# One decoder layer on 256 tokens: TensorE's order written in the source, side work as chains, both token halves on one weight pair, p's projection first

## The chip, the cores and the metric

The kernel runs on one core of a Trainium2 chip. The metric is the device time of one execution in microseconds (us), the median of several runs of the same program; lower is better.

## The reference

One layer of a hybrid decoder, for 256 tokens of width 2048, in float32. Cut to what matters:

```python
h = rms_norm(x, g_mix_pre);  proj = h @ w_in                     # 2048 x 9728
aq, ak, av, hq, hf, hi, hg, gate_a, gate_b = split(proj)
y_attn = sliding_window_attention(rotary(aq), rotary(ak), av, attn_sinks)
o      = hgrn2_recurrence(hq, hf, hi, lb)       # log_f = log(lb + (1-lb) sigmoid(hf)), chunks
y_hgrn = rms_norm(o, hgrn_gnorm) * silu(hg)
merged = sigmoid(gate_a) * (y_attn @ w_attn_branch) + sigmoid(gate_b) * (y_hgrn @ w_hgrn_branch)
x = x + rms_norm(merged @ w_out, g_mix_post)
gate, up = split(rms_norm(x, g_ffn_pre) @ w_gate_up)             # 2048 x 11264
x = x + rms_norm((silu(gate) * up) @ w_down, g_ffn_post)         # 5632 x 2048
ple_gate = sigmoid(rms_norm(x, g_ple_pre) @ w_ple_gate)          # 2048 x 2048
x = x + rms_norm((p @ w_ple_proj) * ple_gate, g_ple_post)        # p is 256 x 256
```

Rotary takes sine and cosine of position times a frequency; the positions come as int32.

## The kernel before, in words

**Products.** The 256 tokens are two halves, c = 0 and 1, of 128 tokens each. An activation is kept transposed (128 rows of the inner dimension by 128 tokens), and a float32 product x @ w is made as three products of the fp32r type, xh·wh + xh·wl + xl·wh, where xh and wh are rounded and xl and wl are the remainders. A weight tile `raw` is a pair of chunks of 128 rows by 512 columns, 512 KB, loaded on SyncE's queue (`weight_load`). `weight_split` makes `wh` on ScalarE (a copy) and `wl` on VectorE (a subtraction). There are 5 buffers for raw and 8 for each of wh and wl. A block of 512 output columns with an inner dimension of 2048 takes 8 such pairs. `products` (L123) runs all 8 pairs for one half, 48 wide matmuls (128 by 512) into one PSUM tile `acc` (four buffers); `block` does half 0, evacuates it, then half 1. The splits of all 8 pairs are thus held until half 1 has used them.

**Order before.** The program is written stage by stage and a scheduler orders each engine's instructions by priority. Splits get a priority of 1000 instructions ahead (AHEAD), the two steps `apply` (residual, norm and new transposes behind w_out and w_down) 3000 (URGENT). Only the first block is pinned (`kept`, `pinned`): there instructions stay in the order of the source.

**Stages.** (1) The first block of w_in (HGRN's forget gate, `hf`), whose products run as pieces of x arrive. Per piece (512 columns of one half): four transposes into `misc`, the gain, hi and lo. `lower_bounds` makes `lb` by a round trip through DRAM (`lbd`), and `oml` is 1 − lb. (2) The other 18 blocks of w_in, the mixer. Beside them run `rotary_tables` (26 small VectorE steps on a tile `rot`, from `posi`, the positions, cast to `posf`), the four HGRN chains `hgrn_core(c, g)` and the four attention chains. An HGRN chain has seven levels: VectorE subtracts two `bT` slices, ScalarE takes Exp, VectorE multiplies by `qT` and `kT`, TensorE multiplies into `misc` (L463, L478, L480), VectorE copies into `scT`; at its end stand the products with `v` (L516, L518) and the sums `o`. (3) The branch products, merged and transposed, and w_out. (4) SwiGLU: for each of 11 column groups j a gate block and an up block; `sg` is silu(gate), times up (L92), then four transposes (L159) and a copy to `actT`. (5) w_down, with the splits of actT. (6) p's projection: w_ple_proj has two chunks of rows, so one pair and 6 wide matmuls per half and 512 columns, each run just ahead of the w_ple_gate block that it is multiplied with; then the last norm and the stores.

PSUM has 8 banks: four acc, two `misc` with tag mt and two with mh. All small matmuls and transposes go to misc. 59 slots of 2 KB per partition hold the rest, handed out in the order of the source. The lines that matter are L123 (`products`), L159 (`transpose4`), L318 (the cast), L81, L84, L88, L89, L92 (the helpers act, tt, ts, stt, through which nearly every ScalarE and VectorE instruction goes).

Of the kernel before, what the change touches and what calls it, by code (L numbers as in the profile page):

```python
# [18 lines left out]
P = 128  # L19
# [10 lines left out]


@with_exitstack
def block_kernel(ctx: ExitStack, tc: tile.TileContext, I, out: bass.AP):
    """256 tokens as two halves of 128 on the partitions; weights stream once.

    A product x @ w is xh@wh + xh@wl + xl@wh, with xh, wh the float32r
    roundings and xl, wl the remainders (exact in float32r).
    """
# [9 lines left out]

    def nm(s):
# [22 lines left out]
    def misc(tag="mt"):  # L72
        return psum.tile([P, NB], F32, tag=tag, bufs=2, name=nm("misc"))

    pinned = [False]

    def kept(ins):
        return tc.keep_in_program_order(ins) if pinned[0] else ins

    def act(o, i, f, **kw):  # L80
        return kept(A.activation(o, i, f, **kw))  # L81

    def tt(o, a, b, op):
        return kept(V.tensor_tensor(o, a, b, op))  # L84

    def ts(o, a, s1, op0, s2=None, op1=None):
        if op1 is None:
            return kept(V.tensor_scalar(o, a, s1, None, op0))  # L88
        return kept(V.tensor_scalar(o, a, s1, s2, op0, op1))  # L89

    def stt(o, a, s, b, op0, op1):
        return kept(V.scalar_tensor_tensor(o, a, s, b, op0, op1))  # L92
# [14 lines left out]
    def weight_split(raw):  # L107
        """hi and lo parts of two k-chunks."""
# [13 lines left out]

    def products(ps, lhs, pairs, start=True, stop=True):  # L123
        n = len(pairs)
        for i, (k, parts) in enumerate(pairs):
            for j, (wh, wl) in enumerate(parts):
                xh, xl = lhs(k + j)
                T.matmul(ps, xh, wh, start=start and i == 0 and j == 0, stop=False)  # L128
                T.matmul(ps, xh, wl, start=False, stop=False)  # L129
                T.matmul(ps, xl, wh, start=False, stop=stop and i == n - 1 and j == 1)  # L130

    def block(w, ks, col, lhs, evac):
        pairs = weight_slab(w, ks, col)
        for c in range(2):
            ps = acc()
            products(ps, lhs[c], pairs)
            evac(c, ps)

    def lookup(groups):
        def f(k):  # L140
            hi, lo = groups[k // 4]
            return hi[:, k % 4, :], lo[:, k % 4, :]
        f.groups = groups
        return f
# [11 lines left out]
    def transpose4(src, tag="mt"):  # L156
        ps = misc(tag)
        for i in range(4):
            T.transpose(ps[:, cols(i)], src[:, cols(i)], ident)  # L159
# [21 lines left out]
    class Normed:  # L181
        """Transposed x * gain as hi and lo parts, and 1 / rms per token."""

        def __init__(self, gcol0):
            self.gcol0, self.groups, self.ss = gcol0, [], small("ss", 4)

        def square(self, g, xt):
            square_sum(self.ss[:, g:g + 1], xt)
# [17 lines left out]
        def done(self):  # L206
            return lookup(self.groups), rstd(self.ss, 4, D)

    def normed(xg, gcol0):
        n = Normed(gcol0)  # L210
        for g in range(4):
            n.square(g, xg[g])
            n.add(xg[g])
        return n.done()

# [1 line left out]
    x2 = I["x"].rearrange("o (c p) d -> (o c) p d", p=P)  # L217

# [6 lines left out]
    nc.sync.dma_start(ident, I["c_ident"])  # L225
    gcol = cst.tile([P, 64], F32, name="gcol")
# [5 lines left out]
    def gain_columns(names, at):  # L232
# [6 lines left out]
        ps = misc("mh")  # L239
        tc.keep_in_program_order(T.transpose(ps[:, :n], row[:n, :P], ident[:n, :n]))  # L240
        tc.keep_in_program_order(V.tensor_copy(gcol[:, at:at + n], ps[:, :n]))
        free(row)

    gain_columns(["g_mix_pre"], 0)
# [14 lines left out]
    dram = ctx.enter_context(tc.tile_pool(name="dram", bufs=1, space=bass.MemoryType.DRAM))  # L259
    lbs, oml = [slot("lb"), slot("lb")], [slot("oml"), slot("oml")]  # L260

    def lower_bounds():
        """Softmax over the two rows of logits, spread to all partitions."""
# [6 lines left out]
        kept(V.reciprocal(lm, lm))  # L270
# [3 lines left out]
        for g in range(2):  # L274
            G.dma_start(lbs[g], lbd[4 * g:4 * g + 4, :].rearrange("c p -> (c p)").partition_broadcast(P))
        free(lrow)

    # first block of w_in, its products as the halves of x arrive
    w_in = I["w_in"].rearrange("o k n -> (o k) n")
    K16 = list(range(16))  # L280
    xin = [[], []]
# [3 lines left out]
    def first_group(g):  # L285
        xin[0].append(load_x(0, g))
        raws = [weight_load(w_in, 4 * g + 2 * i, 5 * NB) for i in range(2)]
        xin[1].append(load_x(1, g))
        norms[0].add(xin[0][g], False)
        pairs = [(4 * g + 2 * i, weight_split(raws[i])) for i in range(2)]  # L290
        norms[1].add(xin[1][g], False)
        return pairs

    pinned[0] = True
    pairs = first_group(0)
    for g in range(4):
        ahead = first_group(g + 1) if g < 3 else None
        if g == 1:
            lower_bounds()
        for c in range(2):  # L300
            products(first[c], lookup(norms[c].groups), pairs, g == 0, g == 3)
# [621 lines left out]
```

## Time and profile before

| what | value |
|---|---|
| median of 3 runs | 1553.84 us (1553.49 to 1553.97) |
| span of the profiled execution | 1552.4 us |
| TensorE busy | 1516.8 us (98%), 7006 records |
| VectorE busy | 889.8 us (57%) |
| ScalarE busy | 786.3 us (51%) |
| GpSimd busy | 24.4 us (2%) |
| moved by DMA | 282.54 MB, mean 182 GB/s |

The profile has a record for each instruction of each engine. Its page gives busy times and groups: a group's row names the line, the engine, the operation, the tiles (out<-in), the shape, how often, busy time and mean duration, then the idle time ahead of the group and what ended it. PEld is TensorE's loading of the stationary side. The time of one run lies 1.44 us above the span. The row of a window gives start and end, its length, TensorE's busy time with the number of records, then the granted clock, the share of the DMA engines and GB/s; asked of all engines it lists PE, PEld, DVE, ACT and POOL in this order. A row of the timeline gives start, duration, engine, line, operation, tiles, shapes and, in brackets, the wait ahead of it with what ended it. A row of the waits gives total us, times and the longest. A float32 matmul leaves two records, an fp32r one or a transpose one.

### The profile page before, as it was taken

Reading aid. Unit: us, or ns where it says so; the run is one execution under the profiler, and the core shown is the slowest. Engines: PE = TensorE matmul, PEld = TensorE weight load, DVE = VectorE, ACT = ScalarE, POOL = GpSimd, SP = SyncE. Lnnn points to the kernel's source line nnn. Section 1 sums busy time; section 2 is a strip of 40 time slices with the busy share of each in tenths; the row PEclk is TensorE's granted clock in tenths of the full one; section 3 lists DMA queues with packets and bytes.
Section 4 is the critical chain, followed back from the end, with each engine's and each line's share of the span. In section 5 each row is a group of like instructions: output and inputs, shape, how many; then the busy total and the mean of one; then the engine's idle time right before and its main releaser. Section 6 shows DMA issues by size and latency. Waiting matters only on the chain.

```text
span 1552.4 us, 18678 instructions
## 1 busy us (share of the span) xinstructions
PE 1516.8 (98%) x7006; PEld 1243.8 (80%) x7006; DVE 889.8 (57%) x1228; ACT 786.3 (51%) x1052; POOL 24.4 (2%) x36
## 2 busy tenths in 40 slices
PE   7999999999999999999999999999999999999997
PEld 5778887887878888887888888888888888888886
DVE  6886748676445565556543553454446556654854
ACT  4755745555664433546443444344345545543852
POOL 2000000000000000000000000000000000000000
PEclk9999999999999999999999999999999999999998
DMA  7645454545336765545545654565565565755452
GB/s 245 230 135 191 129 197 139 187 129 196 110 109 210 247 211 173 193 153 196 200 162 180 217 174 168 200 219 180 172 215 190 190 195 180 246 184 179 171 179 98
DMA packets 146618, 282.54 MB, mean 182 GB/s; under 512 B 9136, under 2 KB 9600, under 8 KB 146528
## 3 DMA queue, kind: packets, MB, share of 16 engines
q1 hardware_dynamic: 145968, 280.33, 54.2%
q0 software_dynamic: 528, 1.01, 0.3%
q8 instruction: 55, 0.90, 0.2%
q14 instruction: 35, 0.29, 0.1%
q10 hardware_dynamic: 32, 0.01, 0.0%
HBM read 279.21 MB, written 2.10 MB: 181 GB/s over the span
## 4 chain that ended last, share of the span: by engine, by line
PE 83%; DMA 6%; ACT 4%; DVE 4%; issue 2%; POOL 0%; SPq 0%; POOLq 0%; ACTq 0%; DVEq 0%
PE acc L130 26%; PE acc L129 26%; PE acc L128 26%; DMA raw<-in_w_gate_up 3%; ACT wh L81 3%; PE misc L159 2%; DMA raw<-in_w_in 2%; DVE wl L84 2%; PE misc L478 1%; PE misc L599 1%; PE misc L617 1%; DVE sg L92 1%; DMA x<-in_x 1%; ACT junk L81 0%; DMA raw<-in_w_down 0%
## 5 line engine op out<-in xcount | busy, mean ns | idle before, releaser
L84 DVE TENSOR_TENSOR wl<-raw,wh 128x1024 fp32r<-128x1024 f32 x516 | 626.7, 1223 | 352.9 <-ACT wh L81 322.4
L129 PE MATMUL acc<-wl,hi 128*128 128x512 f32 x2064 | 809.7, 392 | 1.5 <-DVE wl L84 1.5
L128 PE MATMUL acc<-wh,hi 128*128 128x512 f32 x2064 | 809.4, 392 | 1.2 <-ACT hi L81 0.8
L130 PE MATMUL acc<-wh,lo 128*128 128x512 f32 x2064 | 809.1, 392 | 0.0
L81 ACT ACTIVATE wh<-raw 128x1024 fp32r<-128x1024 f32 x516 | 545.1, 1061 | 254.6 <-PE acc L130 182.1
L128 PEld LDWEIGHTS acc<-wh,hi 128*128 128x128 f32 x2064 | 388.1, 188 | 81.2 <-ACT hi L81 1.1
L129 PEld LDWEIGHTS acc<-wl,hi 128*128 128x128 f32 x2064 | 388.0, 188 | 80.9 <-DVE wl L84 2.1
L130 PEld LDWEIGHTS acc<-wh,lo 128*128 128x128 f32 x2064 | 388.0, 188 | 79.0 <-issue 0.5
L81 ACT ACTIVATE actT<-misc 128x512 f32<-128x512 f32 x22 | 13.2, 598 | 114.1 <-PE misc L159 114.1
L92 DVE SCALAR_TENSOR_TENSOR sg<-acc,rstd,sg 128x512 f32<-128x512 f32 x26 | 19.4, 747 | 77.4 <-PE acc L130 76.1
L81 ACT ACTIVATE sg<-acc,rstd 128x512 f32<-128x512 f32 x26 | 17.7, 681 | 84.1 <-PE acc L130 84.1
L84 DVE TENSOR_TENSOR lo<-actT,hi 128x512 fp32r<-128x512 f32 x44 | 30.2, 688 | 29.1 <-PE acc L129 22.1
L81 ACT ACTIVATE hi<-actT 128x512 fp32r<-128x512 f32 x44 | 27.4, 626 | 35.7 <-PE acc L130 29.8
L81 ACT ACT_TABLE_LOAD x30 | 38.5, 1283 | 2.1 <-PEq L911 1.2
L81 ACT ACTIVATE junk<-acc 128x512 bf16<-128x512 f32 x16 | 9.5, 596 | 56.2 <-DVE yg L84 56.2
L178 POOL TENSOR_TENSOR rstd<-mse,mhalf 128x1 f32<-128x1 f32 (+1 forms) x14 | 13.7, 979 | 1409.0 <-DVE mse L89 1409.0
L84 DVE TENSOR_TENSOR yg<-acc,gp 128x512 f32<-128x512 f32 x16 | 11.0, 686 | 42.7 <-PE acc L130 42.7
L81 ACT ACTIVATE xx<-xx 128x512 f32<-128x512 f32 (+1 forms) x28 | 16.7, 599 | 29.7 <-DVE xx L84 24.9
L81 ACT ACTIVATE gate<-acc,rstd 128x512 f32<-128x512 f32 x16 | 10.9, 681 | 35.1 <-PE acc L130 35.1
L605 DVE CUSTOM_DVE_ANT_0 s<-misc,amask 128x128 f32<-128x128 f32 (+1 forms) x32 | 10.1, 354 | 27.4 <-PE misc L599 27.4
L159 PE MATMUL misc<-ident,x 128*128 128x128 f32 x96 | 15.9, 296 | 8.8 <-DMA x<-in_x 6.7
L159 PEld LDWEIGHTS misc<-ident,x 128*128 128x128 f32 x96 | 11.6, 150 | 13.6 <-DMA x<-in_x 7.2
(157 smaller groups left out, 579.5 us busy)
## 6 DMA issues: line engine op xcount, KB each, us to landing
raw<-in_w_gate_up SPq DMA_DIRECT2D x176, 512.0 KB, 5.1
raw<-in_w_in SPq DMA_DIRECT2D x152, 512.0 KB, 5.1
raw<-in_w_down SPq DMA_DIRECT2D x88, 512.0 KB, 5.5
raw<-in_w_out SPq DMA_DIRECT2D x32, 512.0 KB, 5.5
raw<-in_w_ple_gate SPq DMA_DIRECT2D x32, 512.0 KB, 5.8
raw<-in_w_attn_branch SPq DMA_DIRECT2D x16, 512.0 KB, 5.9
raw<-in_w_hgrn_branch SPq DMA_DIRECT2D x16, 512.0 KB, 5.6
x<-in_x SPq DMA_DIRECT2D x16, 256.0 KB, 6.9
```

What stands on the lines that cost most here:

```text
L81: return kept(A.activation(o, i, f, **kw))
L84: return kept(V.tensor_tensor(o, a, b, op))
L92: return kept(V.scalar_tensor_tensor(o, a, s, b, op0, op1))
L128: T.matmul(ps, xh, wh, start=start and i == 0 and j == 0, stop=False)
L129: T.matmul(ps, xh, wl, start=False, stop=False)
L130: T.matmul(ps, xl, wh, start=False, stop=stop and i == n - 1 and j == 1)
L159: T.transpose(ps[:, cols(i)], src[:, cols(i)], ident)
L178: G.tensor_tensor(r, u, mhalf[:, :m], ALU.pow)
L478: T.matmul(ps[:, cols(h, 64)], xh, blk(xh)[:, :, 1, :], start=True, stop=True)
L599: T.matmul(ps[:, cols(i, nk * P)], qT[:, cols(j0 + i)], kTp[n][:, g, 0:nk * P], start=True, stop=True)
L605: V.tensor_tensor_reduce(s[:, cols(i, nk * P)], ps[:, cols(i, nk * P)], amask[:, (1 - c) * P:256], 1.0, NEG, ALU.add, ALU.max, mx[:, hb + ...
L617: T.matmul(y[:, cols(hb + i, 64)], pT[:, cols(i * nk + b)], vtok[:, b, kv:kv + 64], start=b == 0, stop=b == nk - 1)
```

## The change

1. **TensorE's order.** Each matmul and transpose is kept in the order of the source (`mm`, `transpose`). The other engines stay with the scheduler; the pinning of VectorE and ScalarE at the start, and of the cast of the positions, is gone. `products` and the new `both` advance a `clock` by 0.227 per wide and 0.11 per small matmul.
2. **Chains.** Side work (HGRN, attention, transposes behind an evacuation, apply) becomes generators. `yield d` hands back until TensorE's clock is d further; `pump`, called behind each pair of a half, runs what is due. `hurry(done)` runs waiting chains at once until a condition holds. It stands before the second group of HGRN chains, before the second pair of attention chains, in `lookup`, and where a result is needed.
3. **Both halves on one pair.** `both` runs a pair for half 0 and half 1 before the next pair; `halves_apart` keeps the old order for five blocks: the last of w_out and of w_down, SwiGLU's first gate block, the first and the last of w_ple_gate. The three terms now come as xh·wh, xl·wh, xh·wl.
4. **p's projection first.** Its four blocks open the program. The results are copied out (half 0 on ScalarE, half 1 on VectorE), stored to DRAM `projd` on GpSimd's queue, and loaded again on SyncE's queue among the weights behind w_down's start (the w_ple_gate stage multiplies by them).
5. **Smaller things.** x's first pieces are split chunk by chunk (`by_chunk`: four hi with the gain on ScalarE, four lo on VectorE, 128 by 128) as all later ones were; misc has three buffers with tag mt and one my; the mixer's blocks come in another sequence.

```diff
+    def mm(*a, t=SMALL, **kw):
+        clock[0] += t
+        tc.keep_in_program_order(T.matmul(*a, **kw))
...
+    def pump():
+        while waiting and waiting[0][0] <= clock[0]:
+            _, _, gen, pri = heapq.heappop(waiting)
+            step(gen, pri)
+
+    def hurry(done):
+        while not done():
+            _, _, gen, pri = heapq.heappop(waiting)
+            step(gen, pri)
...
+    def terms(ps, lhs, k, parts, start, stop):
+        xh, xl = lhs(k)
+        wh, wl = parts
+        mm(ps, xh, wh, t=WIDE, start=start, stop=False)
+        mm(ps, xl, wh, t=WIDE, start=False, stop=False)
+        mm(ps, xh, wl, t=WIDE, start=False, stop=stop)
...
+    def both(pss, lhs, w, ks, col, start=True, stop=True):
+        for i, k in enumerate(ks[::2]):
+            (_, parts), = weight_slab(w, [k, k + 1], col)
+            for c in range(2):
+                for j in range(2):
+                    terms(pss[c], lhs[c], k + j, parts[j], start and i == 0 and j == 0,
+                          stop and k + 2 > ks[-1] and j == 1)
+                pump()
...
         posf = small("posf", 2)
-        tc.keep_in_program_order(V.tensor_copy(posf, posi))
+        V.tensor_copy(posf, posi)
...
+    def ev_p(n):
+        def f(c, ps):
+            t = slot("proj")
+            act(t, ps, AF.Copy) if c == 0 else V.tensor_copy(t, ps)
+            G.dma_start(projd[c][n], t)
+            free(t)
+        return f
+
+    for n in range(4):
+        block(w_pp, [0, 1], n * NB, [p_lookup(0), p_lookup(1)], ev_p(n))
+        if n == 1:
+            load_xg(0)
+        if n == 2:
+            add_xg(0)
+    free(*pT)
+    lower_bounds()
+    hT = [lookup(n.groups) for n in norms]
+    for g in range(4):
+        both(first, hT, w_in, [4 * g, 4 * g + 1], 5 * NB, g == 0, False)
+        if g < 3:
+            load_xg(g + 1)
+            add_xg(g + 1)
+        both(first, hT, w_in, [4 * g + 2, 4 * g + 3], 5 * NB, False, g == 3)
...
+        factors(0)
+        for lev in range(7):
+            yield 5.5
+            if lev < 6:
+                factors(lev + 1)
+            scores(lev)
...
     mixer_block(8, evac_hi(1))
     free(*lbs, *oml)
-    hgrn_core(0, 1)
+    hurry(lambda: (1, 0) in hg_o)
+    chain(hgrn(1))
     mixer_block(0, evac_q(0))
...
         def ev_u(c, ps):
-            t = sg[c]
-            stt(t, ps, r2[c], t, ALU.mult, ALU.mult)
-            actT[c][j] = slot("actT")
-            act(actT[c][j], transpose4(t), AF.Copy)
-            free(t)
+            def f():
+                t = sg[c]
+                stt(t, ps, r2[c], t, ALU.mult, ALU.mult)
+                yield 5.0 + c
+                actT[c][j] = slot("actT")
+                act(actT[c][j], transpose4(t), AF.Copy)
+                free(t)
+            chain(f())
...
+    proj = [[slot("proj") for _ in range(4)] for _ in range(2)]
+    for n in range(4):
+        for c in range(2):
+            nc.sync.dma_start(proj[c][n], projd[c][n])
```

How it moves the instructions, at three places. **VectorE at the start of the program**, before (`h`, `lo` belong to x's first pieces, `wl` to w_in):

```order
L241 COPY gcol<-misc_80 128x16
L84 TENSOR_TENSOR h_117<-misc_112,gcol 128x512
L84 TENSOR_TENSOR lo_120<-h_117,hi_119 128x512
L84 TENSOR_TENSOR wl_124<-raw_106,wh_123 128x1024
L84 TENSOR_TENSOR wl_128<-raw_108,wh_127 128x1024
```

and after (`lrow` is the softmax of lower_bounds, `lo_89` and `wl_129` belong to p's projection, `rot` to the rotary tables):

```order
L303 COPY gcol<-misc_94 128x16
L396 CAST posf_891<-posi 128x2
L121 TENSOR_TENSOR lrow_97<-lrow_97 8x128
L125 TENSOR_SCALAR rot_893<-ctri_99,posf_891 128x32
L333 RECIPROCAL lrow_97<-lrow_97 8x128
L121 TENSOR_TENSOR wl_129<-raw_126,wh_128 128x1024
L121 TENSOR_TENSOR lo_89<-misc_83,hi_88 128x512
L121 TENSOR_TENSOR wl_155<-raw_152,wh_154 128x1024
```

The cast stood in row 71 before and stands in row 5 now, ahead of the first split; the rotary steps follow it between the splits and the chunks of x.

**TensorE in the mixer, at the end of the HGRN chain of half 1, first group**, before (`xx` are the factors of levels 4 and 5, acc_1415 is a block of w_in):

```order
L128 MATMUL acc_1415<-wh_1405,hi_292 128x512
L478 MATMUL misc_1303<-xx_1261 128x64 x4
L129 MATMUL acc_1415<-wl_1406,hi_292 128x512
L480 MATMUL misc_1314<-xx_1262 64x64 x4
L130 MATMUL acc_1415<-wh_1405,lo_293 128x512
```

and after (levels 3 to 6, then the first product with `v`):

```order
L60 MATMUL acc_1596<-wl_1756,hi_463 128x512
L60 MATMUL misc_1780<-xx_1578 128x64 x4
L60 MATMUL misc_1791<-xx_1577 128x64 x4
L60 MATMUL misc_1802<-xx_1578 64x64 x4
L60 MATMUL misc_1809<-xx_1577 64x64 x4
L60 MATMUL misc_1822<-v_889,scT_550 128x128
L60 MATMUL misc_1822<-st_1487,xx_1578 128x128
```

The wide matmuls that stood between the levels have gone to other places; these levels wait for nothing but their own chain. Elsewhere in the mixer two levels of a chain have 30 wide matmuls between them.

**TensorE at the end of a SwiGLU block**, before (acc_5951 is the up block of half 1, begun five rows earlier, and sg_5793 belongs to half 0):

```order
L128 MATMUL acc_5951<-wh_5848,hi_5629 128x512
L129 MATMUL acc_5951<-wl_5849,hi_5629 128x512
L159 MATMUL misc_5945<-ident,sg_5793 128x128 x4
L130 MATMUL acc_5951<-wh_5848,lo_5630 128x512
L128 MATMUL acc_5951<-wh_5854,hi_5629 128x512
```

and after (acc_6150 and acc_6151 are the next gate block, sg_5940 is half 0):

```order
L60 MATMUL acc_6151<-wh_6172,lo_5837 128x512
L60 MATMUL acc_6151<-wl_6173,hi_5836 128x512
L64 MATMUL misc_6189<-ident,sg_5940 128x128 x4
L60 MATMUL acc_6150<-wh_6197,hi_5699 128x512
L60 MATMUL acc_6150<-wh_6197,lo_5700 128x512
```

The transposes stood 5 wide matmuls behind half 0's last product and stand 24 behind the block's last one.

More of the change, by code (lines that the diff above doesn't have):

```diff
@@ L1 @@
+import heapq
 import math
@@ L206, in done @@
         def done(self):
[L207 to L214, printed above, removed]
+            hurry(lambda: self.squared == 4)
+            return rstd(self.ss, 4, D)
     x2 = I["x"].rearrange("o (c p) d -> (o c) p d", p=P)
+    dram = ctx.enter_context(tc.tile_pool(name="dram", bufs=1, space=bass.MemoryType.DRAM))
     def load_x(c, g):
@@ L283, in block_kernel @@
     first = [acc(), acc()]
[L285 to L299, printed above, removed]
-        for c in range(2):
-            products(first[c], lookup(norms[c].groups), pairs, g == 0, g == 3)
-        pairs = ahead
@@ L527, in hgrn_core, with hgrn @@
         hg_o[c, g] = o, rstd(ss, 1, P, 4)
+    def hgrn(g):
+        for c in range(2):
+            yield 3.0
+            yield from hgrn_core(c, g)
     def evac_hg(g):
@@ L783, in act_parts @@
     def act_parts(pair, gi):
+        hurry(lambda: all(actT[c][j] is not None for c in range(2) for j in kgroups[gi]))
         parts = [{j: split(actT[c][j]) for j in kgroups[gi]} for c in range(2)]
```

411 lines of the change are left out of this document (237 added, 174 removed).

## The prediction

> **What bounds the kernel now.** I read the page's header and groups first.
>
> ```profile
> span 1552.4 us, 18678 instructions
> PE 1516.8 (98%) x7006; PEld 1243.8 (80%) x7006; DVE 889.8 (57%) x1228; ACT 786.3 (51%) x1052; POOL 24.4 (2%) x36
> L84 DVE TENSOR_TENSOR wl<-raw,wh 128x1024 fp32r<-128x1024 f32 x516 | 626.7, 1223 | 352.9 <-ACT wh L81 322.4
> L129 PE MATMUL acc<-wl,hi 128*128 128x512 f32 x2064 | 809.7, 392 | 1.5 <-DVE wl L84 1.5
> L81 ACT ACTIVATE wh<-raw 128x1024 fp32r<-128x1024 f32 x516 | 545.1, 1061 | 254.6 <-PE acc L130 182.1
> ```
>
> TensorE is the bound: three lines of 2064 wide matmuls (128x512) make 6192. The 392 ns overlap; the pitch comes from the timeline of a full stretch, where six pitches lie between these starts:
>
> ```profile
> 793.27 0.39 PE L129 MATMUL acc<-wl,hi 128*128 128x512 f32 x1
> ...
> 794.63 0.39 PE L129 MATMUL acc<-wl,hi 128*128 128x512 f32 x1
> ...
> 795.38 0.42 PEld L159 LDWEIGHTS misc<-ident,sg 128*128 128x128 f32 x4 [0.78 <-DVE sg L92]
> ```
>
> 1.36 / 6 = 0.2267 us, and 6192 of them are 1404 us. A small matmul into `misc` takes 0.11: two and two more start 0.22 apart.
>
> ```profile
> 317.13 0.38 PE L516 MATMUL misc<-v,scT 128*128 128x128 f32 x2
> ...
> 317.35 0.39 PE L518 MATMUL misc<-st,xx 128*128 128x128 f32 x2
> ```
>
> The change keeps every wide and every small one. The pitch does not depend on which of the three terms follows which, so the new order of the terms is worth 0. What an order can change is TensorE's idle time. I find it by stage, from the windows (first the matmuls into acc, then those into misc):
>
> ```profile
> 13.40:52.75 39.35, 35.65 (x142) 1.00 0.79 264
> 52.75:160.00 107.25, 92.60 (x382) 1.00 0.48 161
> 240.00:480.00 240.00, 197.69 (x789) 1.00 0.44 148
> 480.00:720.00 240.00, 233.22 (x1014) 1.00 0.58 192
> 720.00:1200.00 480.00, 470.53 (x2050) 1.00 0.57 191
> 1200.00:1460.00 260.00, 255.37 (x1119) 1.00 0.60 194
> 1460.00:1541.90 81.90, 81.90 (x363) 1.00 0.45 154
> ```
>
> ```profile
> 52.75:160.00 107.25, 20.40 (x147) 1.00 0.48 161
> 240.00:480.00 240.00, 62.64 (x422) 1.00 0.44 148
> 480.00:720.00 240.00, 9.87 (x64) 1.00 0.58 192
> 720.00:1200.00 480.00, 13.20 (x84) 1.00 0.57 191
> 1200.00:1460.00 260.00, 6.06 (x40) 1.00 0.60 194
> ...
> L599 PE MATMUL misc<-kTp,qTa 128*128 128x256 f32 x32 | 9.3, 386 | 1.2 <-ACT qTa L81 1.2
> ```
>
> Stall of a stage = its length − acc x 0.2267 − misc x 0.11. That gives 4.5 us for 52.75 to 160; 14.7 for 240 to 480, or 11.2 once its 32 scores of 256 columns (L599) are charged 0.22; 3.1 for branches and output projection (480 to 720); 6.1 for SwiGLU (720 to 1200); 1.9 for the down projection (1200 to 1460); nothing for the last 82 us. The whole prize behind the start is thus some 27 us.
>
> **The start.** The program now runs p's projection (48 wide) and then w_in's first block (96) before anything else. Before, those first 144 wide matmuls (2 before 13.4 and 142 in the row above) were done at 52.75. So 52.75 is the mark to beat. The order of VectorE decides it. The cast `posf` from `posi` now stands ahead of the first `wl` of all.
>
> ```profile
> 4.30 0.76 POOL L258 DMA_DIRECT2D posi<-in_positions  x1
> posi<-in_positions POOLq DMA_DIRECT2D x1, 1.0 KB, 7.8
> 12.12 0.78 PE L128 MATMUL acc<-wh,hi 128*128 128x512 f32 x1
> lb<-lbd POOLq DMA_DIRECT2D x2, 256.0 KB, 4.3
> L92 DVE SCALAR_TENSOR_TENSOR lo<-misc,gcol,hi 128x128 fp32r<-128x128 f32 x64 | 19.8, 344 | 4.2 <-ACT hi L81 3.9
> L92 DVE SCALAR_TENSOR_TENSOR rot<-rot 128x64 f32<-128x64 f32 x9 | 1.9, 223 | 0.2
> ```
>
> POOL's queue up to posi is as before: it is issued at 4.3 and lands 7.8 later, at 12.1. With the cast, one row of `rot` and a reciprocal behind it, the first wl starts near 13.6 and the first `lo` of p ends at 13.6 + 1.2 + 0.7 = 15.5. TensorE's second matmul waits for that. Its own work from there (144 x 0.2266, 32 transposes of x x 0.11, a little at the low clock) would end near 53, no later than before. But VectorE cannot keep up. From row 11 of its new order to the last chunk of x's `lo` (row 109) stand 17 wl x 1.223 = 20.8 us, 32 lo x 0.344 = 11.0, four copies of p's projection (no such row before; between a 0.42 and the 0.69 of a 512-wide operation; I take 0.69) 2.8, two `oml` 0.8, 41 rows of rot and rope at about 0.2 = 8.2, and ten of norms at about 0.13 = 1.3: 44.9 us in all. Starting at 15.5 it ends at 60.4 if it never waits. It does wait: the copies for TensorE, `oml` for `lb`, whose loads now stand on POOL's queue among the stores of p's projection (4.3 us to landing), the chunks for ScalarE's `hi`. I put 2.5 us on that: the first block ends at 63, which is **+10 us**. Bounds: 53 (0, if VectorE kept pace) and 75 (+22, if it were busy only 75% of that stretch). Splits of the next block are among these rows, but TensorE's lost time is not got back by having them early.
>
> **The mixer** held 4.5 + 11.2 = 15.7 us. In the new order the levels of HGRN's chains mostly stand 30 wide (6.8 us) apart. Before, the same steps ran in a heap, with wide matmuls between them:
>
> ```profile
> 307.62 1.00 PE L478 MATMUL misc<-xx 128*128 128x64 f32 x8
> ...
> 311.10 1.08 PE L478 MATMUL misc<-xx 128*128 128x64 f32 x8
> ...
> 315.49 0.68 PE L480 MATMUL misc<-xx 128*64 128x64 f32 x8
> ```
>
> From level 3 (307.62) to level 6 (315.49) three steps take 7.9 us there, 2.6 each, so 6.8 us is enough for nearly all. But `hurry` empties the first chain before hgrn(1) enters: levels 3 to 6 of half 1 and the product behind them stand back to back, with nothing wide between. That product began at 317.13 (L516, quoted first), so from level 3 on the chain needed 9.5 us; TensorE's own part is about 2.7 (two such groups of 1.0 and two of 0.7, their overlapping ends taken off), so about 7 us stand still (5 to 10). Then 2.5 us (0 to 5) where the second hf's evacuation meets the end of half 0, because VectorE's rows there add up to about 17 us by the means of their groups where TensorE has about 15 of work. For every other chain I leave 3.5 us, as much as the head of the old chains cost:
>
> ```profile
> PE misc L159 <- ACT bT L81: 3.6, 4, 1.3
> ```
>
> 7 + 2.5 + 3.5 = 13, so **−3 us** (from −8 to +4).
>
> **SwiGLU.** The transposes of a block now stand 24 and 30 wide matmuls behind its last one, 5.4 and 6.8 us; before they stood 5 and 8 behind the last of their half.
>
> ```profile
> PE misc L159 <- DVE sg L92: 3.9, 10, 0.7
> ...
> PE acc L129 <- DVE wl L84: 1.5, 2, 0.8
> ```
>
> The waits name 3.9 us in 10 places for it, the stage shows 6.1; the last sg of a block is done 0.78 us after TensorE's loads began to wait, so with 5 us it always is there: **−5.5 us** (−3.9 to −6.1). The branches' transposes, the chains of the two applies and the down projection hold 3.1 + 1.9 = 5.0 us, of which I take **−3.5** (0 to −5.0): w_out's and w_down's last blocks still run half after half, so half 0's norm lies under half 1's 48 matmuls as before.
>
> **At nothing.** Both halves on one pair: a pair now serves 12 matmuls at once, 2.72 us, against 1.22 us of VectorE and 1.06 of ScalarE for its split; TensorE's waits for wl before are 1.5 us in two places. DMA: 512 KB per 2.72 us is 193 GB/s; 264 GB/s moved at the start. p's projection adds 2 MB of stores on POOL's queue and 2 MB of loads on SP's queue among w_down's weights, where 194 GB/s moved; five raw buffers and eight split pairs lie between queue and TensorE. Without that cover 2 MB would cost 2 / 0.194 = 10 us, and at the very end nothing waits for it. After the last matmul (1541.9) nothing changes: 10.5 us.
>
> **Sum.** 1552.4 + 10 − 3 − 5.5 − 3.5 = 1550.4 us of span. The runs' median of 1553.84 is 1.4 over the profiled span, so **1551.8 us**. A measurement can tell about 0.2% (3.1 us) from no change; this is inside it.
>
> **Rivals.** (1) *Chains in time*: VectorE's rows overlap at their ends and the chunks come before TensorE needs them; the block ends at 57.5 and hurry costs 5: 1551.8 − 5.5 − 2 = 1544.3. For it: many of the small rows are independent. Against it: nothing but order stands between cast, splits and chunks. (2) *VectorE's start falls behind*, slower: if waits in its fixed order leave it busy 80% of the stretch, the block ends at 15.5 + 44.9 / 0.8 = 71.6, 8.6 later than forecast: 1560.4. It decides once the block ends after 68.2 (busy share under 85%). For it: in 13.4 to 52.75 VectorE was busy
>
> ```profile
> 13.40:52.75 39.35, 36.62 (x164) 29.09 (x163) 28.07 (x39) 23.97 (x36) 2.23 (x4) 1.00 0.79 264
> ```
>
> 28.07 of 39.35 us, 71%. Against it: it had less to do then. (3) *The clock falls.* After its long first wait TensorE ran at a pitch of 0.42, and came to 0.22 at about 15.5 (the granted clock of the windows reads 1.00 there too, so the pitch has to show it):
>
> ```profile
> 14.40 0.63 PE L128 MATMUL acc<-wh,hi 128*128 128x512 f32 x1
> ...
> 14.82 0.61 PE L129 MATMUL acc<-wl,hi 128*128 128x512 f32 x1
> ...
> 15.51 0.39 PE L128 MATMUL acc<-wh,hi 128*128 128x512 f32 x1
> ...
> 15.73 0.39 PE L129 MATMUL acc<-wl,hi 128*128 128x512 f32 x1
> ```
>
> From 12.12 to 15.5 that lost about half, 1.7 us. No later wait before exceeds 1.3 us; if two stalls of the new order (the start, hurry) were long enough to drop the clock again, 2 x 1.5 = 3 us come on top: 1554.8. The Trainium skill, "TensorE: Matmul & The Clock Gate", Part 1, states such a gate: half clock after about 3.4 us without work, full again after about 3.4 us of work; it speaks against packing dependent rows with nothing between, and by it the price would be an estimated 1.7 us a gap. The rows above agree with the warm-up; no row before shows a fall later on.
>
> **Chances.** Forecast 0.40 (1547 to 1557), rival 1 0.25, rival 2 0.27, rival 3 0.08. Faster by over 0.2% (under 1550.7): rival 1 and 0.17 of the forecast, 0.42. Within 0.2%: 0.23 of the forecast and rival 3, 0.31. Slower: 0.27. The range goes from the start at no cost (1541.8) to a VectorE busy 75% there (block's end at 75.4: 1564.2); the forecast alone spans 1547 to 1557.
>
> **What would show it.** In the changed profile: the first 144 wide matmuls end near 63 and TensorE's waits at the start name VectorE's lo and wl; one stretch of about 11 us in the mixer with no acc matmul between five misc groups; no wait for sg in SwiGLU, a stage stall there under 1 us; a pitch of 0.22 to 0.23 everywhere behind 19 us. Wrong if the block ends before 57 or after 68, if SwiGLU keeps over 2 us of stall, or if w_down shows waits for proj or raw.

## The result, and the profile after

The changed kernel takes 1582.86 us (median of 4 runs, 1580.27 to 1583.53) against 1553.9 us for the kernel before: 1.0175 times as long, 95% interval 1.016 to 1.0191. The forecast was 1551.8 us with a range to 1564. The profiled execution took 1580.27 us, 2.2 over its span; it is the fastest of the four.

The head of the page after, and of its 40 slices (39.5 us each) TensorE's busy tenths and its granted clock:

```profile
span 1578.1 us, 18723 instructions
PE 1521.9 (96%) x7006; PEld 1260.5 (80%) x7006; DVE 889.0 (56%) x1248; ACT 789.7 (50%) x1070; POOL 24.7 (2%) x44
...
PE   5999989999999999997999999999999999999897
...
PEclk9999989999999999998999999999999999999999
```

Slices 6 and 19 (from 197 and from 710 us) show less work and a lower clock together, slice 38 (from 1460) and the first less work. The waits of TensorE after:

```profile
PE misc L64 <- DVE x L129: 14.3, 2, 8.1
PE acc L60 <- DVE lo L129: 6.2, 4, 4.4
PE acc L60 <- DVE lo L121: 5.1, 1, 5.1
PE acc L60 <- ACT hi L118: 4.0, 1, 4.0
...
PE misc L60 <- DVE xx L121: 3.4, 2, 3.0
PE misc L64 <- DVE kTp L682: 3.3, 2, 2.0
```

The work is the same (7006 records); TensorE waits more, and for VectorE. The two waits for `x`, 14.3 us together, are new: the residual that is transposed behind w_out and behind w_down. No wait for `sg` is left. (Each row: total, times, longest.)

The windows by stage, with TensorE's wide matmuls, cut where each stage's last one has begun (96 or 144 in the first, 1728 in the mixer, 384 in the branches, 384 in w_out, 2112 in SwiGLU, 1056 in w_down, the rest; a record or two at an edge is counted twice). After:

```profile
0.00:66.42 66.42, 40.42 (x144) 0.95 0.81 265
66.42:547.37 480.95, 414.64 (x1730) 0.99 0.54 160
547.37:637.12 89.75, 87.86 (x386) 1.00 0.67 209
637.12:726.49 89.37, 88.16 (x386) 1.00 0.56 167
726.49:1227.49 501.00, 487.53 (x2114) 0.99 0.65 191
1227.49:1468.72 241.23, 240.46 (x1058) 1.00 0.63 198
1468.72:1567.49 98.77, 90.49 (x386) 0.97 0.44 141
```

And before, by the same stages:

```profile
0.00:39.30 39.30, 24.96 (x96) 1.00 0.75 247
39.30:519.07 479.77, 418.73 (x1730) 1.00 0.49 163
519.07:610.38 91.31, 89.01 (x386) 1.00 0.69 223
610.38:700.64 90.26, 87.84 (x386) 1.00 0.53 178
700.64:1198.05 497.41, 485.88 (x2113) 1.00 0.56 188
1198.05:1441.14 243.09, 240.19 (x1058) 1.00 0.61 196
1441.14:1542.15 101.01, 99.28 (x434) 1.00 0.46 157
```

The second number of a row is the stage's length; that is where to read. p's 48 wide matmuls (10.9 us) moved from the last stage to the first. Put at the same place they leave: start 66.42 − 39.30 − 10.9 = +16.2, mixer +1.2, branches −1.6, w_out −0.9, SwiGLU +3.6, w_down −1.9, w_ple_gate 98.77 − 101.01 + 10.9 = +8.7, the tail +0.4. The sum is the 25.7 us by which the span grew. Two stages that should have gained have lost, SwiGLU and w_ple_gate, both at their head. This is the timeline behind w_out's last block, which ends at 726.5 (VectorE's and TensorE's rows that matter):

```profile
729.60 0.40 PE L60 MATMUL acc<-wl,hi 128*128 128x512 f32 x1
...
734.75 0.68 DVE L121 TENSOR_TENSOR yg<-acc,gp 128x512 f32<-128x512 f32 x1
...
737.26 2.74 DVE L129 SCALAR_TENSOR_TENSOR x<-yg,rstd,x 128x512 f32<-128x512 f32 x4 [0.67 <-POOL rstd L240]
738.07 1.11 PE L64 MATMUL misc<-ident,x 128*128 128x128 f32 x4 [8.08 <-DVE x L129]
...
739.84 0.63 PE L60 MATMUL acc<-wl,hi 128*128 128x512 f32 x1
740.26 0.63 PE L60 MATMUL acc<-wh,hi 128*128 128x512 f32 x1
```

And before, where that block ended at 700.6:

```profile
706.73 0.68 DVE L84 TENSOR_TENSOR yg<-acc,gp 128x512 f32<-128x512 f32 x1
...
709.23 2.08 DVE L92 SCALAR_TENSOR_TENSOR x<-yg,rstd,x 128x512 f32<-128x512 f32 x3 [0.66 <-POOL rstd L178]
710.04 0.66 PE L159 MATMUL misc<-ident,x 128*128 128x128 f32 x4 [0.92 <-DVE x L92]
```

VectorE was late before, too: half 1's `yg` came 6.1 us behind the block's end, because four splits and six chunks of half 0's `lo` ran on VectorE first; after it is 8.3, with four splits and nine chunks. But before, 36 wide matmuls of the next block stood ahead of half 1's transposes, and TensorE lost 0.92 us. Now 12 stand there, and it loses 8.08, and then starts again at a pitch of 0.42 us (739.84 to 740.26). Of the 7.2 us between the two waits, 24 wide matmuls are 5.4; the later `yg` is about the rest.

### The profile page after: what moved, and what is told of

It is laid out like the page before. It is cut to its first block, busy times and chain, and to the rows that moved or that the text cites. A ratio compares the mean times of both kernels' runs of the same rounds, so it can differ in the third digit from the quotient of the medians.

```text
span 1578.1 us, 18723 instructions
## 1 busy us (share of the span) xinstructions
PE 1521.9 (96%) x7006; PEld 1260.5 (80%) x7006; DVE 889.0 (56%) x1248; ACT 789.7 (50%) x1070; POOL 24.7 (2%) x44
## 3 DMA queue, kind: packets, MB, share of 16 engines
q1 hardware_dynamic: 147120, 282.43, 59.1%
## 4 chain that ended last, share of the span: by engine, by line
PE 92%; DVE 3%; issue 2%; DMA 1%; ACT 1%; POOL 0%; SPq 0%; POOLq 0%; DVEq 0%; ACTq 0%
PE acc L60 86%; PE misc L60 3%; PE misc L64 2%; DVE wl L121 1%; DMA lb<-lbd 1%; ACT wh L118 0%; DVE lo L129 0%; DMA raw<-in_w_gate_up 0%; DVE xx L121 0%; ACT junk L118 0%; DMA raw<-in_w_ple_proj 0%; DMA raw<-in_w_ple_gate 0%; DVE x L129 0%; ACT hi L118 0%; DVE eg L129 0%
## 5 line engine op out<-in xcount | busy, mean ns | idle before, releaser
L60 PE MATMUL acc<-wh,hi 128*128 128x512 f32 x2064 | 820.5, 398 | 4.0 <-ACT hi L118 4.0
L118 ACT ACTIVATE hi<-misc,gcol 128x128 fp32r<-128x128 f32 x96 | 32.9, 364 | 27.4 <-DVE lo L129 23.5
L129 DVE SCALAR_TENSOR_TENSOR lo<-misc,gcol,hi 128x128 fp32r<-128x128 f32 x96 | 31.4, 346 | 15.8 <-ACT hi L118 15.6
L240 POOL TENSOR_TENSOR rstd<-mse,mhalf 128x1 f32<-128x1 f32 (+1 forms) x14 | 9.6, 687 | 1460.9 <-DVE mse L126 1460.9
L64 PE MATMUL misc<-ident,x 128*128 128x128 f32 x96 | 16.3, 304 | 14.6 <-DVE x L129 14.3
L60 PEld LDWEIGHTS misc<-xx 128*128 128x128 f32 (+1 forms) x192 | 21.4, 180 | 6.0 <-ACT xx L118 2.8
L60 PE MATMUL misc<-xx 128*128 128x64 f32 (+1 forms) x192 | 22.2, 263 | 3.0 <-ACT xx L118 2.7
L121 DVE TENSOR_TENSOR xx<-bT 128x256 f32<-128x256 f32 x52 | 20.1, 420 | 8.3 <-PE misc L60 5.6
```

The source lines that it names most:

```text
L60: tc.keep_in_program_order(T.matmul(*a, **kw))
L64: tc.keep_in_program_order(T.transpose(o, i, idn))
L118: return A.activation(o, i, f, **kw)
L121: return V.tensor_tensor(o, a, b, op)
L129: return V.scalar_tensor_tensor(o, a, s, b, op0, op1)
L240: G.tensor_tensor(r, u, mhalf[:, :m], ALU.pow)
```

## The experiments

Fourteen kernels; each is the changed kernel with the edit shown. A ratio is to the kernel before, run beside it.

| run | us | ratio, 95% interval | start's end | mixer | SwiGLU | w_ple_gate |
|---|---|---|---|---|---|---|
| changed | 1582.86 | 1.0175 (1.016 to 1.0191) | 66.4 | 481.0 | 501.0 | 98.8 |
| e1_rot_later | 1572.9 | 1.0106 (1.0083 to 1.013) | 58.1 | 481.1 | 501.1 | 98.8 |
| e2_half1_later | 1576.44 | 1.0127 (1.0104 to 1.015) | 66.3 | 483.4 | 496.5 | 96.7 |
| e3_hurry_later | 1581.54 | 1.0159 (1.0131 to 1.0186) | 65.8 | 484.5 | 500.1 | 98.5 |
| e4_swiglu_near | 1582.39 | 1.0166 (1.0142 to 1.019) | 66.4 | 483.1 | 500.3 | 98.8 |
| e5_half0_close | 1580.13 | 1.0152 (1.0137 to 1.0167) | 66.2 | 483.1 | 498.7 | 96.7 |
| e6_rot_oml_later | 1574.18 | 1.0111 (1.0094 to 1.0127) | 57.6 | 484.2 | 500.7 | 98.6 |
| e7_swiglu_at_once | 1590.39 | 1.0212 (1.0192 to 1.0232) | 69.3 | 483.5 | 506.6 | 97.9 |
| e8_p_last | 1582.36 | 1.0166 (1.0151 to 1.0182) | 52.3 (96 wide) | 483.6 | 501.1 | 112.3 (with p) |
| e9_whole_pieces | 1575.73 | 1.0118 (1.0082 to 1.0155) | 60.9 | 483.9 | 500.8 | 98.5 |
| e10_half1_spread | 1572.01 | 1.0098 (1.0064 to 1.0132) | 67.1 | 482.9 | 500.7 | 90.9 |
| e11_mixer | 1570.63 | 1.0092 (1.0061 to 1.0122) | 65.9 | 471.8 | 500.7 | 99.0 |
| e12_all | 1555.42 | 0.9993 (0.998 to 1.0007) | 60.9 | 471.6 | 499.1 | 90.8 |
| e13_three | 1554.05 | 0.9988 (0.9979 to 0.9996) | 58.5 | 471.7 | 499.4 | 90.7 |
| e14_squares | 1551.96 | 0.997 (0.9958 to 0.9983) | 59.1 | 473.2 | 497.5 | 91.7 |

The last four columns are stage lengths in the profiled execution, cut as above. Where the edit does not touch them, the start (65.8 to 69.3) and the mixer (481.0 to 483.6) move by up to 3.5 us from run to run, so a smaller change of theirs alone shows nothing; SwiGLU (500.1 to 501.1) and w_ple_gate (97.9 to 99.0) move by about 1 us. The kernel before took 1553.9 us beside the changed kernel and 1556.1 to 1557.2 beside the others, so a difference in us between rows of this table is uncertain by some 3 us, and a stage's length says more. The theory at the outset, A: TensorE's fixed order waits wherever its input is late, and the loss is the sum of a few such places. The rival, B: it is spread (the halves side by side, the order of the terms, the clock).

**The start.**

```diff
+        ts(posf, hg_k[1, 0][:, :2], 0.0, ALU.mult)
         V.tensor_copy(posf, posi)
```

> The rotary tables get one more input: the first block's k tile, so the cast and all of their small steps can only come behind the first block. Theory A (TensorE's fixed order waits wherever VectorE is late, so the loss is the sum of a few places): at the start VectorE loses about 5 us to the wait for the positions ahead of the first split and 8 us to the steps of rot and rope; the first 144 wide matmuls end at 54 to 58 instead of 66.4, and the run is 9 us (6 to 12) shorter than the changed kernel's 1582.9, about 1574. Theory B (the loss is spread: the new order of terms and halves, or a lower clock, costs something everywhere): the order of a few small VectorE steps changes little, 0 to 3 us.

Measured: 8.3 us shorter at the start, 10.0 us in all. Theory A. The edit moves the cast and the small steps together; 4.9 of the 8.3 us are there by TensorE's second wide matmul, which starts at 10.07 instead of 14.92, and are thus the cast's wait. In the changed kernel's start these rows of VectorE show what stood in the way:

```profile
11.84 0.17 DVE L396 CAST posf<-posi 128x2 f32<-128x2 int32 x1 [6.62 <-DMA posi<-in_positions]
...
13.13 1.15 DVE L121 TENSOR_TENSOR wl<-raw,wh 128x1024 fp32r<-128x1024 f32 x1
...
28.85 0.43 DVE L126 TENSOR_SCALAR oml<-lb 128x512 f32<-128x512 f32 x1 [4.35 <-DMA lb<-lbd]
```

The cast held the first split until 13.13, though ScalarE's half of it was done at 8.5 (wh from 7.43, 1.06 long).

```diff
-            ts(oml[g], lbs[g], -1.0, ALU.mult, 1.0, ALU.add)
...
+    for g in range(2):
+        ts(oml[g][:, :1], r1[1], 0.0, ALU.mult)
+        ts(oml[g], lbs[g], -1.0, ALU.mult, 1.0, ALU.add)
```

> The rotary tables come later as in the first of the runs, and oml gets one more input, so that VectorE no longer stops for lb (4.35 + 1.22 us in the changed kernel) among the first splits. Theory A: the first 144 wide end some 3 us sooner than the 58.1 of the run with rot alone, and the run is 2 to 5 us under its 1572.9, about 1569. Rival: with rot gone the rows behind oml wait for TensorE and ScalarE anyway: 0 to 1 us.

Measured: the start 0.5 us shorter than with rot alone, the run 1.3 us longer, intervals overlapping. The rival holds: once the rotary steps are gone, the 4.35 us of waiting for `lb` delay nothing that TensorE wants next.

```diff
-            norms[c].add(xin[c][g])
+            norms[c].add(xin[c][g], False)
```

> The rotary tables come later, as in the first of the runs, and x's first pieces are split whole as before the change (gain, hi and lo of 512 columns at once) and not chunk by chunk. Theory A (ScalarE's and VectorE's many short rows keep the start long: four hi of 0.365 us per piece instead of one of 0.63 is 6.6 us of ScalarE over 8 pieces): the first 144 wide end at 53 to 55 instead of 58.1, the run is 3 to 5 us under 1572.9, about 1569. Rival (x's landing or the splits themselves set the end): 0 to 1 us.

Measured: the start 2.8 us longer, not shorter (60.9 against 58.1; intervals of the runs overlap). ScalarE's sum fell, but a whole piece is a chain of three steps (gain, hi, lo) before its first chunk can be used, and TensorE's waits for hi in the start went from 3.5 to 9.1 us. Theory A's reason here, the sum of ScalarE's rows, was wrong. Whether such chains are also what remains of the start's loss is not shown.

```diff
-    for n in range(4):
-        block(w_pp, [0, 1], n * NB, [p_lookup(0), p_lookup(1)], ev_p(n))
-        if n == 1:
-            load_xg(0)
-        if n == 2:
-            add_xg(0)
-    free(*pT)
+    load_xg(0)
+    add_xg(0)
...
     for n in range(4):
+        block(w_pp, [0, 1], n * NB, [p_lookup(0), p_lookup(1)], ev_p(n))
         block(w_pg, K16, n * NB, h3T, ev_s(n), n in (0, 3))
```

> p's projection goes back to where it was before the change, one block ahead of each w_ple_gate block, without the copies to DRAM; all else as changed. Theory A (VectorE bounds the start): 8 us of VectorE work leave the start (four wl, lo of p, four copies), its stall falls from 29.7 to 20 to 23 us and the run is 6 to 9 us shorter, about 1575. Rival (the start waits for the positions, lb and x, and p's products only fill that time): the start's stall stays at 27 to 30, and the run is unchanged, about 1583.

Measured: no difference (1.0166 against 1.0175). The rival holds: the start's 96 wide now end at 52.3 and w_ple_gate's stage grows by 13.5 us, 10.9 of them p's products. Doing p's projection first neither helps nor harms here; it fills time in which VectorE works on x.

**The two applies.**

```diff
-                    yield 2.8 if g == 0 else 1.9
+                    yield (2.8 if g == 0 else 1.9) if c == 0 else (9.6 if g == 0 else 0.4)
```

> Behind the last block of w_out and of w_down the transposes of half 1 enter 9.6 us behind the block's end (then 0.4 apart) instead of 2.8 (1.9 apart); half 0 stays. Theory A: TensorE does half 0 of the next block meanwhile; the two stalls of 11.2 us (SwiGLU's stage) and 9.1 us (w_ple_gate's stage) fall to about 2 each, the run is 16 us (13 to 18) shorter, about 1567. Theory B: half 1 is late anyhow and its products wait instead of its transposes: the stalls only move by 9 us, the run is 0 to 5 us shorter.

Measured: 6.4 us shorter, between the two theories. SwiGLU's stage gained 4.5 us, w_ple_gate's 2.1. The wait for x fell from 14.3 us to 0.9, but a wait of 4.0 us for `lo` between two of half 1's transposes behind w_down (four stand in a row there, and misc has three buffers with their tag) and several short ones for half 1's chunks took its place.

```diff
-                    yield 2.8 if g == 0 else 1.9
+                    yield (2.8 if g == 0 else 0.3) if c == 0 else (9.6 if g == 0 else 0.4)
```

> As the run with half 1's transposes later, and half 0's behind the same two blocks now stand 0.3 apart instead of 1.9. Theory A1 (VectorE's order holds half 1's yg behind half 0's last chunks, which wait for half 0's widely spaced transposes): yg comes some 4 us sooner, the two stages' stalls fall from 6.7 and 7.0 to 2 to 3 each, the run is 8 us shorter than the 1576.4 of that run, about 1568. Theory A2 (VectorE simply has more work there, two sets of 16 chunks and 8 splits, than TensorE's order leaves it time): no change within 2 us, about 1576.

Measured: 3.7 us longer than e2, though the intervals of the two ratios overlap, with more waits, ten for `lo` (9.1 us) and four for `hi` (8.4 us). The stages of w_out (91.1 against 89.4 us) and SwiGLU are longer by 1.8 and 2.2. Theory A1 is out: counted from the start of its stage, half 1's yg comes only 0.5 us sooner behind w_out and 0.8 us later behind w_down, so half 0's spacing is not what holds it back.

```diff
-                    yield 2.8 if g == 0 else 1.9
+                    yield (2.8, 1.9, 1.9, 1.9)[g] if c == 0 else (9.0, 1.3, 2.6, 2.6)[g]
```

> Behind w_out and w_down half 1's transposes enter at 9.0, then 1.3, 2.6 and 2.6 us further, so that the last two stand among half 1's own products; half 0 as in the changed kernel. Theory A (what is left of the stall with 9.6 and 0.4 is four sets of chunks wanted at once from ScalarE and VectorE): the two stages' stalls fall from 6.7 and 7.0 to 2 to 4 each, the run is 6 to 9 us under 1576.4, about 1569. Rival (VectorE has too much work there in any order): 1574 to 1578.

Measured: 10.9 us under the changed kernel, but one-sided. Behind w_down the stage went from 98.8 to 90.9 us, 1.2 us over its 89.7 us of work (384 x 0.2267 and 24 transposes). Behind w_out the stage stayed at 500.7: the wait for x fell there from 8.08 to 1.33 us, but waits for hi and lo came in its place. ScalarE's rows around half 1's first hi read:

```profile
742.11 0.63 ACT L118 ACTIVATE junk<-x 128x512 bf16<-128x512 f32 x1
...
742.74 0.35 ACT L118 ACTIVATE hi<-misc,gcol 128x128 fp32r<-128x128 f32 x1
742.99 0.62 ACT L118 ACTIVATE junk<-x 128x512 bf16<-128x512 f32 x1
...
743.60 0.35 ACT L118 ACTIVATE hi<-misc,gcol 128x128 fp32r<-128x128 f32 x1
743.97 1.28 ACT L118 ACT_TABLE_LOAD   x1
745.27 0.69 ACT L118 ACTIVATE sg<-acc,rstd 128x512 f32<-128x512 f32 x1
745.86 0.62 ACT L118 ACTIVATE hi<-misc,gcol 128x128 fp32r<-128x128 f32 x2
```

A square of the new x stands between half 1's first two hi, and a table load for Silu and half 0's sg between the second and the third.

**SwiGLU.**

```diff
-                yield 5.0 + c
+                yield 0.8 + c
```

> In SwiGLU the transposes enter 0.8 and 1.8 us behind a block's end instead of 5 and 6. Theory A: with the order fixed TensorE waits for the last sg each time, 1 to 2 us in each of 11 blocks: 11 to 22 us longer, about 1597. Theory B (SwiGLU's stall of 6 us went because both halves share a weight pair, not because of the distance): 0 to 4 us longer.

Measured: no difference. Chains are taken up only behind a pair of a half, so 0.8 and 1.8 both came out 6 wide matmuls (1.4 us) behind the block's last product, where the profile has all eight transposes in a row; that is 12 behind half 0's last product and 6 behind half 1's. A distance of 1.4 us is enough.

```diff
-                yield 5.0 + c
...
+                yield 0.0
             chain(f())
```

> In SwiGLU the transposes of both halves stand directly behind the block's last product, with no wide matmul between. Theory A (a fixed order waits for what it is given too early): each of 11 block ends waits for Silu's product on VectorE, some 2 us: 20 us longer than the changed kernel, about 1603. Theory B (the shared weight pair took SwiGLU's stall away): under 5 us longer.

Measured: 7.5 us longer, between the two theories. SwiGLU's stage is 5.6 us over that of the changed kernel, and w_down's, at whose head the last block's transposes now stand, 2.2 over (243.4 us). That is 0.7 us per block, far less than the 2 expected (half 0 ends 6 wide matmuls ahead of half 1), but it is the size of the stall before the change, and TensorE's weight loads wait for sg again (22 times, 9.9 us). Theory A in kind: the shared pair alone does not take SwiGLU's stall away, the distance is needed. Whether the distance would do it without the shared pair, no run shows.

**The mixer.**

```diff
+    mixer_block(0, evac_q(0))
     hurry(lambda: (1, 0) in hg_o)
     chain(hgrn(1))
-    mixer_block(0, evac_q(0))
```

> The hurry and the second group of HGRN chains stand behind the block of the first q instead of ahead of it, 96 wide matmuls later. Theory A: the four levels get their distance, the stall of about 8 us at 220 to 231 goes, 5 to 8 us shorter, about 1576. Theory B: the second group starts one block later and is then hurried where its output gate wants it, so the stall comes back there: 0 to 2 us shorter.

Measured: within the noise (1.0159 against 1.0175). The rest of the chain was still hurried, one wait of 3.6 us for scT, 27 us later.

```diff
-            yield 5.5
+            yield 4.0
...
                 transpose(pt[:, cols(i)], m1[:, cols(i)], ident)
+            for i in range(2):
                 for g in range(2):
```

> In the mixer HGRN's levels stand 4.0 us apart instead of 5.5, so the first group's chains end before the hurry has anything to do, and the two key transposes of a half stand ahead of both pairs of copies. Theory A: the stalls at the hurry (about 5 us with the low clock behind it) and at the key transposes (3.6) go: 7 to 10 us shorter, about 1574. Rival (at 4.0 us VectorE's and ScalarE's part of a level comes late and TensorE waits a little at each of 28 levels): no gain or longer, 1583 to 1590.

Measured: 12.2 us shorter, the mixer 471.8 us, 9.2 shorter. With levels 18 wide apart (4.1 us) instead of 30, nothing is left for the hurry, and the levels are not late: of the mixer's waits one for `xx` (3.4 us) and one for wh (1.2 us) remain.

```profile
PE misc L60 <- DVE xx L121: 3.4, 1, 3.4
...
PE misc L60 <- ACT wh L118: 1.2, 1, 1.2
```

**Together.** The rotary steps later, whole pieces, half 1 spread and the mixer's edit:

> The four edits together: rotary later, whole pieces, half 1 spread, levels at 4.0 with the key transposes ahead. Theory A: the parts add up: 1582.9 - 10 - 4 - 14 - 8 = 1547, under the kernel before the change. If VectorE's load in each place is what counts and waits move on instead of going: 1560 to 1570, still over 1553.8.

Measured: 1555.42 us, level with the kernel before (0.998 to 1.0007). The parts that were measured alone are −10.0 + 2.8 (whole pieces) − 10.9 − 12.2 = −30.3; the whole is −27.4. So they do add up, nearly. The stages show it more sharply: start (60.9), mixer (471.6) and w_ple_gate (90.8) have the lengths that they had in the runs of their own edits.

> The edits that helped, together: rotary later, half 1 spread, the mixer's levels at 4.0 with the key transposes ahead; x's first pieces chunk by chunk as in the changed kernel (the whole pieces made the start's stall 24.1 us instead of 21.4). If the parts add up, 2.8 us under the 1555.4 of the run with all four, about 1552.6, level with the kernel before (1553.8) or just under it; if the start's length is set by something else, 1555.

Measured: 1554.05 us, 0.9988 (0.9979 to 0.9996); the start is back at 58.5. The time lies between the two that were expected; the start's stage fell by 2.4 us, near the 2.8.

```diff
                     stt(xr[c][g], yg[c][g], r, xr[c][g], ALU.mult, ALU.add)
                     free(yg[c][g])
+                    if c == 0:
+                        norm.square(g, xr[c][g])
...
-                chain(squares())
+                if c == 1:
+                    chain(squares())
```

> As the run of three edits, and the squares of half 0's new x run on ScalarE as soon as each piece is there, not in a chain behind all four transposes. If what is left at the start of SwiGLU (9 to 11 us even with half 1 spread) is ScalarE's queue, where six squares, a table load and sg stand ahead of half 1's hi, the stall there falls to 4 to 6 us and the run is 4 to 6 us under the run of three, about 1548. Rival (the loads of w_gate_up or VectorE's splits set it): 0 to 1 us.

Measured: 1551.96 us, 0.997 (0.9958 to 0.9983), 0.3% under the kernel before (1556.14 us beside it) and well under the changed one. SwiGLU's stage is 1.9 us shorter than in the run of three edits and the run 2.1 us: less than expected, and the ratios' intervals touch (0.9979 and 0.9983), so that ScalarE's squares are a part of what holds half 1 there is likely, not shown. Some 8 us over its work (478.7 us of wide matmuls and 11.0 of small ones) remain in that stage; what sets them is open.

## Why the prediction was wrong, step by step

**The step that failed: the applies.** "The branches' transposes, the chains of the two applies and the down projection hold 3.1 + 1.9 = 5.0 us, of which I take −3.5 (0 to −5.0): w_out's and w_down's last blocks still run half after half, so half 0's norm lies under half 1's 48 matmuls as before." That is right of half 0. Of half 1, whose norm lies under nothing but the next block, it says nothing. The term's bound on its bad side was 0, so a loss there was put at nothing. But the stall before was small because 36 wide matmuls stood ahead of the transposes; 12 do now. Branches, w_out and w_down did gain 4.4 us (1.6 + 0.9 + 1.9), a little more than forecast. The two ends lost 9.3 (SwiGLU's +3.6 with its own gain of 5.7 taken out: 6.1 of stall before, 0.4 after) and 8.7 us. So the term came to +13.6 instead of −3.5, 17.1 of the 27.7 us by which the span missed the forecast's 1550.4. The start has 6.2 of them (+16.2 against +10), the mixer 4.2. None of the signs that I had named as wrong looked at these two places. The rows were there to be counted, and the 0.92 us in the trace of before was no price for the new distance: a price was the 9.4 us from the block's end (700.64) to the transposes (710.04), less 12 x 0.2267 = 2.7 us, so 6.7 us a place. The rest, up to the 9 us lost, is the later yg and the low clock behind the wait.

The runs bear this out behind w_down: with half 1's transposes spread (e10) 7.9 of the 8.7 us went. Behind w_out they do so in part: 4.5 us went in e2, none in e10, 1.6 to 3.5 in the runs of several edits. There, moving the transposes moves the wait to hi, lo and the products behind them; what sets the rest is open.

**The start: the place right, the size under-estimated.** Forecast +10 us with the block's end at 63; it ended at 66.4, +13.7 against the mark of 52.75. (By the stages above it is +16.2, since before the mixer's first 48 wide matmuls took 13.45 us and not 10.9; counted from that mark the mixer has the other 2.5.) Rows 11 to 109 of VectorE's order ran from 14.8 to 65.9. The window from my 15.5 on:

```profile
15.50:65.92 50.42, 42.08 (x173) 32.54 (x171) 39.47 (x106) 35.09 (x69) 7.09 (x13) 0.93 0.81 267
```

VectorE (third pair) was busy for 39.5 us, not 44.9, since short rows overlap, and it waited 11 us, not 2.5: 78% busy, close to the share of rival 2. That rival put the block's end 8.6 us behind the forecast; with less busy time it came 3.4 behind. The cast and the rotary steps are half of the loss (e1: −8.3 at the start); the loads of lb are not behind it (e6), nor p's projection (e8). What the other 7.9 us are (58.1 − 39.3 − 10.9) no run shows.

**The mixer: −3 forecast, +1.2 measured**, inside the term's bounds (−8 to +4). The hurry was priced rightly. Its rows:

```profile
221.01 1.00 PE L60 MATMUL misc<-xx 128*128 128x64 f32 x8
...
226.12 1.95 PE L60 MATMUL misc<-xx 128*64 128x64 f32 x16 [2.73 <-ACT xx L118]
...
232.90 0.77 PE L60 MATMUL acc<-wh,hi 128*128 128x512 f32 x1
```

In 11.9 us TensorE does 48 small matmuls, 5.3 us by 0.11 each, so 6.6 us are lost where I had 7: 4.1 in waits (0.30, 2.73, 0.67 and 0.38); the granted clock there is 0.54 (225.0 to 235.2). The key transposes, 3.3 us of waits, were not in my sum: the source makes TensorE wait for a copy between two transposes, which the scheduler had not done. e11 took both away, 9.2 us of the mixer with the low clock behind them, with two small edits.

**SwiGLU: right.** Forecast −5.5; behind the first 16 us the stage has no stall left. The row holds 2093 wide and 92 small matmuls, by 0.2267 and 0.11 484.6 us of its 484.99:

```profile
742.50:1227.49 484.99, 480.56 (x2093) 1.00 0.65 191
```

**At nothing: right.** The stores and loads of p's projection show in no wait of w_down, whose stage got shorter, and the order of the terms changes no pitch.

**The clock: rival 3 happened, besides the rest.** I gave it 0.08 and 3 us. In the changed kernel 36 wide matmuls in seven places, each behind a wait of TensorE, follow one another at 0.42 to 0.43 us (nine from 15.5 on, eight from 739.4 on, for example): 36 x 0.2 = 7 us, against three such matmuls in a row before. It is contained in the stage lengths above. The granted clock of the stretch behind w_out shows it:

```profile
726.49:742.50 16.01, 6.97 (x23) 0.70 0.58 190
```

The Trainium skill ("TensorE: Matmul & The Clock Gate", Part 1) states half the clock after a window of about 3.4 us without work. This trace agrees in kind: 8.1 us of waiting brought eight slow matmuls, and the wait of 3.0 us that ended at 185.0 brought none. But a window wholly without work is not needed here: two waits of 2.0 and 1.2 us (ended at 144.1 and 145.8), with two transposes between them, brought six.

## What to carry to other kernels

When an order is taken from a scheduler and fixed, price each dependent step by the time from its producer's start to its arrival in the old trace, less the work that the new order puts between, and not by the wait that the old trace shows: that wait is what was left after the scheduler had filled it. (Here this gives 6.7 us a place and about 9 were lost: the low clock and a later producer come on top.) Do it for each half or copy by itself, since only the last one has no sibling's work to hide under. And fixing one engine's order leaves the others to the scheduler, which may put early whatever it takes to be ready (here a cast that waits 6.6 us for a small load) in front of what the fixed engine wants first.

## What the runs showed of the hardware

The low clock is paid for in pieces: after a wait TensorE needed 0.4 to 1.8 us more for the next 2 to 9 wide matmuls. Which waits set it off varied from run to run. The same wait of 3.0 us for `xx` in the mixer ended at 185.0 us in the changed kernel and at 185.1 in e4, and behind it the granted clock was full in the one (first row) and half in the other (second row):

```profile
186.00:189.00 3.00, 3.00 (x20) 1.00 0.81 238
...
186.00:189.00 3.00, 3.00 (x15) 0.50 0.79 238
```

It may be a part of why the mixer's length moved from 481.0 to 483.6 us with the same code there. Loads of 512 KB landed in 3.7 us (median) where before they took 5.1 (raw's row of w_gate_up in the list of DMA issues); little time could come of that, since TensorE's waits for splits, which need raw, were 1.9 us in all before (wl 1.5, wh 0.4).
